# Loading x ahead of the small constants, and splitting four channel blocks at a time, in a hybrid trunk kernel

## The chip, the cores and the metric

The kernel runs on one core of a Trainium2 chip. The time is the device time of one execution in microseconds (us); the median of several executions counts. The profile names the engines PE (matmul; PEld its weight loads), DVE (vector), ACT (activation), POOL and SP. SP here does little but issue DMAs.

## The reference

One layer of an encoder, on x of 1024 tokens by 1024 channels, in fp32. Three head groups share one input projection; their results go through one output projection, and a gated feed-forward follows.

```python
h = rmsnorm(x, pre_mix_norm[l])
proj = h @ w_in[l]
(a_q, a_k, a_v, s_z, s_xbc, s_dt, g_qkv, g_z, g_b, g_a) = jnp.split(proj, offs, axis=-1)
att = swa_sink_alibi(a_q, a_k, a_v, attn_sinks[l])
ssd = ssd_mixer(s_z, s_xbc, s_dt, ssd_conv_w[l], ssd_conv_b[l], ...)
gdn = gdn_mixer(g_qkv, g_z, g_b, g_a, gdn_conv_w[l], gdn_dt_bias[l], gdn_A_log[l], gdn_norm_w[l])
mix = jnp.concatenate([att, ssd, gdn], axis=-1) @ w_out[l]
x = x + rmsnorm(mix, post_mix_norm[l])
h = rmsnorm(x, pre_ffn_norm[l])
f = (jax.nn.silu(h @ ffn_w_gate[l]) * (h @ ffn_w_up[l])) @ ffn_w_down[l]
...
```

`rmsnorm` divides each row by the root of its mean square and multiplies channel by channel with a weight. `gdn_mixer` and `ssd_mixer` run q, k, v and x, B, C through a causal convolution of four taps and SiLU, and form decays exp of cumulated sums from g_a and s_dt.

## The kernel before

The 1024 tokens go through the mixers in two halves of 512 (four tiles of 128 rows, t = 0 to 3). A half's normed rows are turned so that channels lie on partitions: eight blocks (k = 0 to 7) of 128 channels by 512 tokens. Every fp32 operand of the large products is split into a rounded part and a rest (names with `hhi` and `hlo` for activations, `wh` and `wl` for weights, `wr` for the raw weights), and three matmuls stand for one product (`gemm`, `gemm_rows`, L203 to L215).

The opening (`load_norm(0)`, L290 to L321) loads x tile by tile, squares and sums each row on ACT (L253), takes the power -1/2 on POOL (`rsq`, L167), scales the row on DVE (L317), and `split_T` transposes 32 pieces on PE (L231, `tp_a`), multiplies them by the norm's weight as a column (`ncol`, itself turned on PE at L120) and splits them, a block at a time, with 24 ACT (L236) and 24 DVE instructions (L237). `STEPS` has tiles 0 and 1 go alone and 2 and 3 together. Then `load_rest` loads the small constants from SP's queue: masks, biases, norm weights (`nw_in`), and the convolution taps (`cw_gdn`, `cw_ssd`), which PE turns into `pt_conv` (L158) and ACT copies to `wconv` (L159).

The first half then runs the steps of `ORD[0]`. K begins with `decay_block`: `gate_rows` makes `mm_gz`, 96 matmuls of 272 columns, and a chain of small instructions turns the decay inputs into `da`, `cs_ps`, `cs`, `chl`, `tp_cs`, `csT` and then, per pair of tiles, `D_g`, `D_s` and the exponentials `E_g`, `E_s` (L453). Then `conv_block` runs for gk, gq, gk, gq: a product of 24 matmuls of 512 columns into one of two PSUM banks `mm`, its copy `cb_` (L344), an ACT instruction that scales it by the last tap (L348, it needs `wconv`) into `kq`, three DVE multiply-adds (L350), tanh and product. mm_gv, mm_B, mm_C, mm_x and mm_z follow. Step N, late in the half, normalises the second half's rows, whose x has been loaded and scaled in the opening.

A scheduler orders each engine's instructions at build time, in the priority of the code, and `tc.high_priority()` moves a weight piece's load and split forward. An engine then takes its instructions strictly in that order. Buffers come from pools with a fixed number of tiles: `cb` has two, `wr` three, `nat` four, `mm` two banks.

Of the kernel before, what the change touches and what calls it, by code (L numbers as in the profile page):

```python
# [8 lines left out]
F32 = mybir.dt.float32  # L9
# [7 lines left out]
P = 128  # L17
# [16 lines left out]
STEPS = (1, 1, 2)  # L34
# [35 lines left out]
def trunk(ctx, tc, a):  # L70
# [47 lines left out]
    def load_columns():  # L118
        pt = mx("pt_ncol", "gd")
        pe.transpose(pt[:, 0:8], nw8[:, 0:P], ident[0:8, 0:8])  # L120
        vec.tensor_copy(ncol[:, 0:8], pt[:, 0:8])

    def load_rest():
# [6 lines left out]
        dma(row12[:, 0, 4:12], a["ssd_dt_bias"].to_broadcast([P, 8]))  # L130
        dma(row12[:, 0, 0:4], a["gdn_dt_bias"].to_broadcast([P, 4]))
        dma(row12[:, 1, 4:12], a["ssd_A_log"].to_broadcast([P, 8]))
        dma(row12[:, 1, 0:4], a["gdn_A_log"].to_broadcast([P, 4]))
        dma(dskip, a["ssd_D"].to_broadcast([P, 8]))
        dma(sinks, a["attn_sinks"].to_broadcast([P, 4]))
# [3 lines left out]
        dma(nw[0:8, 0:P], a["pre_ffn_norm"][0].rearrange("(k p) -> k p", p=P))  # L139
        dma(nw[10:14, 0:P], a["ssd_norm_w"][0].rearrange("(k p) -> k p", p=P))  # L140
        for i in range(4):
            dma(nw[14 + i // 2:15 + i // 2, (i % 2) * 64:(i % 2 + 1) * 64], a["gdn_norm_w"])
# [5 lines left out]
        for nm, b0, c0 in (("gdn", 8, 0), ("gdn", 11, 384), ("ssd", 0, 0), ("ssd", 4, 512)):  # L148
            n = 3 if nm == "gdn" else 4
            cw = cpool.tile([P, HT + 3], F32, tag="cb", name=f"cw_{nm}{c0}")  # L150
            if nm == "gdn":
                pool.memset(cw[0:5, 0:n * P], 0.0)
            dma(cw[0:4, 0:n * P], a[f"{nm}_conv_w"][0][:, c0:c0 + n * P])
            if nm == "ssd":
                dma(cw[4:5, 0:n * P], a["ssd_conv_b"][:, c0:c0 + n * P])
# [17 lines left out]

    def split_piece(name, n, width, hi, lo, fill):
# [4 lines left out]
        with tc.high_priority():  # L179
            raw = wpool.tile([P, WC], F32, tag="wr", name=f"wr_{name}")  # L180
# [35 lines left out]

    def split_alloc(name, hp):
        return [(hp.tile([P, HT], F32R, tag="hhi", name=f"hhi_{name}{k}", bufs=KB),
                 hp.tile([P, HT], F32R, tag="hlo", name=f"hlo_{name}{k}", bufs=KB))
                for k in range(KB)]  # L220
# [69 lines left out]
    def load_norm(h):  # L290
        def load(t):
            xt = npool.tile([P, D], F32, tag="nat", name=f"x_{h}{t}")
            r0 = h * HT + t * P
            dma(xt, x_in[r0:r0 + P])
            return xt

        xts = []
        with tc.high_priority():
            for t in range(NT):
                if h == 0 and t == 2:  # L300
                    break
                xts.append(load(t))
                if h == 0 and t == 0:
                    dma(nw8[:, 0:P], a["pre_mix_norm"][0].rearrange("(k p) -> k p", p=P))
        for t in range(len(xts), NT):
            xts.append(load(t))
        hT = split_alloc(f"a{h}", hpool)
        if h == 0:
            load_columns()
        t0 = 0  # L310
        for step in STEPS if h == 0 else (NT,):
            nats = []
            for xt in xts[t0:t0 + step]:
                r = rms_scale(xt)
                for g in range(2):
                    s = slice(g * HT, (g + 1) * HT)
                    vec.tensor_scalar(xt[:, s], xt[:, s], r, None, op0=ALU.mult)  # L317
# [55 lines left out]

    def decay_block(h, hT):
# [416 lines left out]
    def half(h, hT, order):  # L791
# [3 lines left out]
        def keys():  # L795
            sc = st["sc"] = decay_block(h, hT)
            kq = [kqpool.tile([P, 2, HT], F32, tag="kq", name=f"kq{h}{b}") for b in range(2)]
            for b in range(2):
                conv_block(h, hT, f"gk{b}", O_G + 256 + b * P, 10 + b, kq[b][:, 0])
                conv_block(h, hT, f"gq{b}", O_G + b * P, 8 + b, kq[b][:, 1])  # L800
            st["grp"] = []
# [57 lines left out]
        def after():  # L859
            st["next"] = load_norm(h + 1)  # L860
# [101 lines left out]

    hT = load_norm(0)
    load_rest()
    for h in range(2):
        for t in range(GT):
            dma(vds[h][t].rearrange("h (b r) j -> (h b r) j", b=4).rearrange("(x r) j -> x r j", r=32)[:, 16:32, 0:16],
                S_bd[0:16].rearrange("p b l -> p (b l)")[:, 0:256].rearrange("p (r j) -> p r j", r=16))
# [398 lines left out]
```

## Time and profile before

| | us |
|---|---|
| median of three runs | 1269.42 |
| lowest and highest | 1267.31, 1270.78 |
| the profiled execution, its time | 1268.95 |
| its span in the trace | 1267.2 |
| PE busy | 1218.1 |
| DVE busy | 913.7 |
| ACT busy | 574.8 |
| POOL busy | 217.8 |

The span runs from the first to the last instruction; 1.75 us of the execution lie outside. A line of the trace gives start and duration, the engine, the line of code, the operation with the tiles that it writes and reads, and in brackets how long the engine had been idle and who released it. L-numbers in the profile are those of the kernel that ran.

### The profile page before, as it was taken

What the parts mean: (1) busy time and instruction counts of PE and PEld (TensorE: products, weight loads), DVE (VectorE), ACT (ScalarE), POOL (GpSimd) and SP (SyncE); (2) the same over time, 40 slices, a digit from 0 to 9 for tenths busy, and PEclk for the clock granted to TensorE, in tenths of its full rate; (3) what the DMA queues carried; (4) which work ended last, traced back from release to release, by engine and by line L of the source; (5) the groups of instructions that cost most, each with busy time, mean ns of one, the idle gap of its engine ahead of it and who ended that gap; (6) DMA issues with size and microseconds to landing.
All of it is one profiled execution on the core that took longest, in us unless ns stands there. A gap on an engine that the chain in (4) does not pass through costs nothing.

```text
span 1267.2 us, 18619 instructions
## 1 busy us (share of the span) xinstructions
PE 1218.1 (96%) x6384; PEld 1005.0 (79%) x6384; DVE 913.7 (72%) x1850; ACT 574.8 (45%) x1245; POOL 217.8 (17%) x313
## 2 busy tenths in 40 slices
PE   5999999999998999889999999999999999999997
PEld 4878778987787889878877888888888887888885
DVE  5677865796797385654668999886677666768885
ACT  7464435456443453553546443333433334444661
POOL 3244454233355432100000000000000000000000
PEclk9999989999998999979999999999999999999998
DMA  7333432143333222464573554542333367676315
GB/s 224 94 78 63 102 78 70 49 117 92 73 90 68 85 86 73 126 224 127 161 232 103 191 190 164 182 155 72 117 108 108 108 244 271 188 238 205 94 57 199
DMA packets 181795, 168.15 MB, mean 133 GB/s; under 512 B 52510, under 2 KB 137018, under 8 KB 181700
## 3 DMA queue, kind: packets, MB, share of 16 engines
q1 hardware_dynamic: 164276, 133.14, 36.0%
q10 hardware_dynamic: 17424, 33.82, 7.3%
q8 instruction: 50, 0.82, 0.3%
q14 instruction: 45, 0.37, 0.1%
HBM read 126.82 MB, written 40.11 MB: 132 GB/s over the span
## 4 chain that ended last, share of the span: by engine, by line
PE 82%; DVE 8%; DMA 6%; ACT 2%; issue 1%; SPq 1%; POOL 0%; ACTq 0%; DVEq 0%; POOLq 0%
PE mm_p L1238 5%; PE mm_p L1239 5%; PE mm_p L1240 5%; DMA wr_e<-in_ffn_w_gate_dram 1%; DMA x<-in_x_dram 1%; PE mm_o L208 1%; PE gram L490 1%; PE mm_o L209 1%; DMA yb<-in_ffn_w_down_dram 1%; PE mm_o L207 1%; PE y L703 1%; PE as L746 1%; PE ao L782 1%; PE mm_z L207 1%; DVE Tpr L538 1%
## 5 line engine op out<-in xcount | busy, mean ns | idle before, releaser
L167 POOL TENSOR_TENSOR rsq<-ssv,mhalf 128x1 f32<-128x1 f32 x32 | 20.0, 628 | 750.9 <-DVE ssv L260 740.3
L208 PE MATMUL mm_z<-wl_z,hhi_a 128*128 128x256 f32 x128 | 37.3, 291 | 1.6 <-DVE wl_z L184 1.6
L207 PE MATMUL mm_z<-wh_z,hhi_a 128*128 128x256 f32 x128 | 38.8, 303 | 0.0
L209 PE MATMUL mm_z<-wh_z,hlo_a 128*128 128x256 f32 x128 | 37.3, 291 | 0.0
L208 PE MATMUL mm_o<-wl_wo,hhi_m 128*128 128x256 f32 x128 | 36.7, 287 | 0.0
L209 PE MATMUL mm_o<-wh_wo,hlo_m 128*128 128x256 f32 x128 | 36.3, 284 | 0.0
L207 PE MATMUL mm_o<-wh_wo,hhi_m 128*128 128x256 f32 x128 | 36.3, 284 | 0.0
L183 ACT ACTIVATE wh_wo<-wr_wo 128x512 fp32r<-128x512 f32 x30 | 18.7, 631 | 27.2 <-PE mm_o L1133 8.2
L184 DVE TENSOR_TENSOR wl_wo<-wr_wo,wh_wo 128x512 fp32r<-128x512 f32 x22 | 15.2, 692 | 18.0 <-ACT wh_wo L183 17.9
L208 PEld LDWEIGHTS mm_z<-wl_z,hhi_a 128*128 128x128 f32 x128 | 25.6, 200 | 2.1 <-DVE wl_z L184 1.9
L207 PEld LDWEIGHTS mm_z<-wh_z,hhi_a 128*128 128x128 f32 x128 | 25.7, 201 | 0.7
L703 PE MATMUL y<-xs,E_s 128*128 128x64 f32 x128 | 19.1, 290 | 7.3 <-DVE E_s L696 7.3
L215 PE MATMUL mm_x<-hhi_a,wl_x 128*128 128x512 f32 x64 | 26.0, 406 | 0.0
L214 PE MATMUL mm_x<-hlo_a,wh_x 128*128 128x512 f32 x64 | 25.5, 398 | 0.0
L209 PEld LDWEIGHTS mm_z<-wh_z,hlo_a 128*128 128x128 f32 x128 | 25.4, 199 | 0.0
L213 PE MATMUL mm_x<-hhi_a,wh_x 128*128 128x512 f32 x64 | 25.3, 395 | 0.0
L703 PEld LDWEIGHTS y<-xs,E_s 128*128 128x128 f32 x128 | 18.1, 208 | 8.7 <-DVE E_s L696 7.7
L208 PEld LDWEIGHTS mm_o<-wl_wo,hhi_m 128*128 128x128 f32 x128 | 24.1, 189 | 1.0 <-issue 1.0
L209 PEld LDWEIGHTS mm_o<-wh_wo,hlo_m 128*128 128x128 f32 x128 | 24.1, 189 | 0.3 <-issue 0.3
L207 PEld LDWEIGHTS mm_o<-wh_wo,hhi_m 128*128 128x128 f32 x128 | 24.1, 188 | 0.3 <-ACT apT L772 0.3
L1131 PE MATMUL mm_o<-wh_wo,mhi 128*128 128x512 f32 x56 | 22.0, 393 | 0.3 <-ACT mhi L236 0.3
L207 PE MATMUL mm_gz<-wh_gz,hhi_a 128*128 128x272 f32 x64 | 20.8, 325 | 1.3 <-ACT dtn L378 1.3
(1801 smaller groups left out, 4380.8 us busy)
## 6 DMA issues: line engine op xcount, KB each, us to landing
wr_wo<-in_w_out_dram SPq DMA_DIRECT2D x32, 256.0 KB
x<-in_x_dram SPq DMA_DIRECT2D x8, 512.0 KB
wr_x<-in_w_in_dram SPq DMA_DIRECT2D x16, 256.0 KB
wr_z<-in_w_in_dram SPq DMA_DIRECT2D x16, 256.0 KB
res<-in_x_dram SPq DMA_DIRECT2D x8, 512.0 KB
resf<-x1d SPq DMA_DIRECT2D x8, 512.0 KB
mixn<-mixd SPq DMA_DIRECT2D x12, 256.0 KB
wr_e<-in_ffn_w_gate_dram SPq DMA_DIRECT2D x12, 256.0 KB
```

Source lines behind the costliest of these rows:

```text
L167: pool.tensor_tensor(r[:, 0:n], v, mhalf[:, 0:n], op=ALU.pow)
L207: pe.matmul(ps, hi[:, tsl], whi, start=k == 0, stop=False)
L208: pe.matmul(ps, hi[:, tsl], wlo, start=False, stop=False)
L209: pe.matmul(ps, lo[:, tsl], whi, start=False, stop=k == len(wp) - 1)
L213: pe.matmul(ps, whi, hi, start=k == 0, stop=False)
L214: pe.matmul(ps, whi, lo, start=False, stop=False)
L215: pe.matmul(ps, wlo, hi, start=False, stop=k == len(wp) - 1)
L703: pe.matmul(yd[:, j], E[j], xs[:, j], start=True, stop=True)
L1131: pe.matmul(ps[t], hi[:, s], whi, start=k == korder[0], stop=False)
L1238: pe.matmul(ps[j], ah[:, s], bh, start=i == 0, stop=False)
L1239: pe.matmul(ps[j], ah[:, s], bl, start=False, stop=False)
L1240: pe.matmul(ps[j], al[:, s], bh, start=False, stop=i == NP - 1)
```

## The change

Six things change.

First, `load_first` replaces `load_norm(0)`. The four x tiles go to buffers that only later stages use, all four are loaded ahead of the weights, and the norm's weight is loaded as a row, broadcast to all partitions (`pn_row`, two of 256 KB). A row is multiplied by its own scale and by that row in one DVE instruction, in place. Four blocks of a tile are transposed into one PSUM tile, one ACT copy makes `hhi` and one DVE subtraction `hlo`, 8 each instead of 24. The split tiles hold four blocks each, everywhere (`split_alloc`, `xtile`).

Second, the second half's x is loaded and scaled in step N; a copy of one column from a tile of the V step holds it back.

Third, the gz weights of the first half use the `nat` buffers, and the weight pieces of K in the first half are not moved forward (`ahead`, `raw_of`).

Fourth, `load_rest` and the eight clears `vd` are called after gz, from `decay_block`.

Fifth, in `load_rest` the biases, norm weights and taps are issued from POOL's queue, 17 DMAs.

Sixth, `STEPS` goes.

```diff
     def load_rest():
+        dma(nw8[:, 0:P], a["pre_mix_norm"][0].rearrange("(k p) -> k p", p=P))
         pt = mx("pt_ncol", "gd")
...
-        dma(row12[:, 0, 4:12], a["ssd_dt_bias"].to_broadcast([P, 8]))
+        nc.gpsimd.dma_start(row12[:, 0, 4:12], a["ssd_dt_bias"].to_broadcast([P, 8]))
...
         pool.memset(nw[0:16, 0:P], 1.0)
-        dma(nw[0:8, 0:P], a["pre_ffn_norm"][0].rearrange("(k p) -> k p", p=P))
+        nc.gpsimd.dma_start(nw[0:8, 0:P], a["pre_ffn_norm"][0].rearrange("(k p) -> k p", p=P))
...
-            dma(cw[0:4, 0:n * P], a[f"{nm}_conv_w"][0][:, c0:c0 + n * P])
+            nc.gpsimd.dma_start(cw[0:4, 0:n * P], a[f"{nm}_conv_w"][0][:, c0:c0 + n * P])
...
-        with tc.high_priority():
-            raw = wpool.tile([P, WC], F32, tag="wr", name=f"wr_{name}")
+        with ahead[0]():
+            raw = raw_of[0](f"wr_{name}")
...
+        hi, lo = [[hp.tile([P, 4, HT], F32R, tag=tg, name=f"{tg}_{name}{k}", bufs=2) for k in range(2)]
+                  for tg in ("hhi", "hlo")]
+        four[:] = [hi, lo]
+        return [(hi[k // 4][:, k % 4], lo[k // 4][:, k % 4]) for k in range(KB)]
...
+    def load_first():
+
+        rows = [rpool.tile([P, HT], F32, tag=f"row{g}", name=f"pn_row{g}") for g in range(2)]
+        xts = []
+        for t in range(NT):
+            xt, start = load_x(t, mpool, ("sE", "Wst")[t // 2], 2)
+            with tc.high_priority():
+                start()
+                if t == 1:
+                    for g in range(2):
+                        dma(rows[g], a["pre_mix_norm"][:, g * HT:(g + 1) * HT].to_broadcast([P, HT]))
+            xts.append(xt)
+        hT = split_alloc("a0", hpool)
+        hi, lo = four
+        for t, xt in enumerate(xts):
+            with tc.high_priority():
+                r = rms_scale(xt)
+                s = slice(t * P, (t + 1) * P)
+                for g in range(2):
+                    q = xt[:, g * HT:(g + 1) * HT]
+                    stt(out=q, in0=q, scalar=r, in1=rows[g], op0=ALU.mult, op1=ALU.mult)
+                    p = mx(f"tp_a{t}{g}", ("gd", "sd", "at", "mm")[(2 * t + g) % 4]).rearrange("p (k c) -> p k c", k=4)
+                    for k in range(4):
+                        pe.transpose(p[:, k], q[:, k * P:(k + 1) * P], ident)
+                    act(out=hi[g][:, :, s], in_=p, func=AF.Copy)
+                    vec.tensor_tensor(lo[g][:, :, s], p, f32(hi[g][:, :, s]), op=ALU.subtract)
+        return hT
...
+            xt, start = load_x(h * NT + t, npool, "nat")
+            vec.tensor_copy(xt[:, 0:1], hold[:, 0:1])
+            start()
...
+        usual = raw_of[0]
+        if h == 0:
+            raw_of[0] = lambda nm: npool.tile([P, D], F32, tag="nat", name=nm)
         gz = gate_rows(h, hT, "gz", [(0, w_in[:, O_GZ:O_GZ + 264]), (264, w_in[:, O_DT:O_DT + 8])], 272,
                        lambda t, ps: act(out=dtn[:, t, :], in_=ps[:, 256:272], func=AF.Copy))
+        raw_of[0] = usual
+        if h == 0:
+            load_rest()
+            clear_inverse()
...
-            st["next"] = load_norm(h + 1)
+            st["next"] = load_norm(h + 1, st["v"][0])
...
-    hT = load_norm(0)
-    load_rest()
+    hT = load_first()
     hT = half(0, hT, ORD[0])
```

The order in which instructions stand on an engine shows where things went. On PE before, between the end of the first mm_gq and the second mm_gk there is nothing; the numbers in the names tell tiles apart.

```order
L213 MATMUL mm_gq00_659<-hhi_a07_191,wh_gq004_653 128x512
L214 MATMUL mm_gq00_659<-hlo_a07_192,wh_gq004_653 128x512
L215 MATMUL mm_gq00_659<-hhi_a07_191,wl_gq004_654 128x512
L213 MATMUL mm_gk10_706<-hhi_a00_177,wh_gk100_694 128x512
L214 MATMUL mm_gk10_706<-hlo_a00_178,wh_gk100_694 128x512
```

On PE after, these stand at the same place, from the last matmul of mm_gq to the first of the second mm_gk (xN: N alike in a row).

```order
L216 MATMUL mm_gq00_619<-hhi_a01_181,wl_gq004_614 128x512
L475 MATMUL D_g000_749<-mask_r_95,ident_r_94 128x512
L142 MATMUL pt_ncol2_460<-cst_90,nw_in_452 128x16
L156 MATMUL pt_conv_464<-cst_90,cw_gdn0_465 128x5 x3
L446 MATMUL cs_ps0_532<-da0_530,cst_90 128x48
L465 MATMUL tp_cs0_551<-cst_90,chl0_548 24x128 x4
L479 MATMUL D_g000_749<-csT0_556,sel_r_96 128x256 x2
L479 MATMUL D_s0001_1801<-csT0_556,sel_r_96 128x256 x2
L156 MATMUL pt_conv_464<-cst_90,cw_gdn384_471 128x5 x3
L156 MATMUL pt_conv_464<-cst_90,cw_ssd0_477 128x5 x4
L156 MATMUL pt_conv_464<-cst_90,cw_ssd512_484 128x5 x4
L214 MATMUL mm_gk10_666<-hhi_a00_180,wh_gk100_654 128x512
```

The masks of D_g and D_s, pt_ncol2 and pt_conv stood inside gz before; cs_ps, tp_cs and the products with csT stood after the second mm_gk had begun. In between, and not shown, stand the further masks and products of the same kind.

On ACT before, the first mm_gk's bank is emptied (cb_gk, kq) right behind the splits of the next weights; D_g's exponentials come some twenty instructions later.

```order
L394 ACTIVATE e0_547<-ay0_545 128x48
L183 ACTIVATE wh_gk104_700<-wr_gk104_702 128x512
L183 ACTIVATE wh_gq100_741<-wr_gq100_743 128x512
L344 ACTIVATE cb_gk00_637<-mm_gk00_612 128x512
L348 ACTIVATE kq00_598<-mm_gk00_612,wconv_98 128x512
```

On ACT after, the decay chain and 16 exponentials stand ahead of it; wconv, which before was copied inside gz, is copied between.

```order
L184 ACTIVATE wh_gv000_1019<-wr_gv000_1021 128x512
L454 ACTIVATE ecs0_538<-cs0_535 128x48
L467 ACTIVATE csT0_556<-tp_cs0_551 24x512
L484 ACTIVATE E_g00_748<-D_g000_749,ncs0_537 128x128 x4
L484 ACTIVATE E_g00_748<-D_g001_757,ncs0_537 128x128 x4
L484 ACTIVATE E_s000_1792<-D_s0000_1793,ncs0_537 128x128 x4
L484 ACTIVATE E_s000_1792<-D_s0001_1801,ncs0_537 128x128 x4
L362 ACTIVATE cb_gk00_597<-mm_gk00_572 128x512
L157 ACTIVATE wconv_98<-pt_conv_464 128x70
L362 ACTIVATE cb_gq00_644<-mm_gq00_619 128x512
L366 ACTIVATE kq00_558<-mm_gk00_572,wconv_98 128x512
```

On POOL, which issued no DMA before, these stand after the split of the second mm_gk's weights. Six other DMAs (biases, A_log, D, sinks) stand at POOL's start, and between the last three rows, not shown, stand the DMAs of cw_gdn384 and cw_ssd512's taps and one product.

```order
L136 MEMSET nw_in_452 16x128
L137 DMA nw_in_452<-in_pre_ffn_norm_dram 8x128
L138 DMA nw_in_452<-in_ssd_norm_w_dram 4x128
L140 DMA nw_in_452<-in_gdn_norm_w_dram 1x16x4 x4
L150 MEMSET cw_gdn0_465 5x384
L185 TENSOR_TENSOR wl_gq100_702<-wr_gq100_703,wh_gq100_701 128x512
L151 DMA cw_gdn0_465<-in_gdn_conv_w_dram 4x384
L185 TENSOR_TENSOR wl_gv000_1020<-wr_gv000_1021,wh_gv000_1019 128x512
L150 MEMSET cw_gdn384_471 5x384
L151 DMA cw_ssd0_477<-in_ssd_conv_w_dram 4x512
L153 DMA cw_ssd0_477<-in_ssd_conv_b_dram 1x16x32
L153 DMA cw_ssd512_484<-in_ssd_conv_b_dram 1x16x32
```

What SP issued in the opening before, ahead of the second half's x, is now issued by POOL around and after the first mm_gk; the tap buffers come from the two `cb` tiles, so each load there waits until PE has read the one before it.

More of the change, by code (lines that the diff above doesn't have):

```diff
@@ new lines, in load_norm @@
+    def load_norm(h, hold):
+        nats = []
+        for t in range(NT):
+            xt, start = load_x(h * NT + t, npool, "nat")
+            vec.tensor_copy(xt[:, 0:1], hold[:, 0:1])
+            start()
+            r = rms_scale(xt)
+            for g in range(2):
+                s = slice(g * HT, (g + 1) * HT)
+                vec.tensor_scalar(xt[:, s], xt[:, s], r, None, op0=ALU.mult)
+            nats.append(cols_of(xt))
+        hT = split_alloc(f"a{h}", hpool)
+        split_T(f"a{h}", nats, 0, hT, 0)
@@ L795, in keys @@
         def keys():
+            if h == 0:
+                ahead[0] = ExitStack
             sc = st["sc"] = decay_block(h, hT)
@@ L800, in keys @@
                 conv_block(h, hT, f"gq{b}", O_G + b * P, 8 + b, kq[b][:, 1])
+            ahead[0] = tc.high_priority
             st["grp"] = []
```

72 lines of the change are left out of this document (25 added, 47 removed).

## The prediction

> **What bounds the kernel now.** I read the page first, then PE's waits in the opening, then windows there, then the order of PE's own instructions. On the page, PE is busy 96% of the span, and of 40 slices only the first is far from full.
>
> ```profile
> span 1267.2 us, 18619 instructions
> PE 1218.1 (96%) x6384; PEld 1005.0 (79%) x6384; DVE 913.7 (72%) x1850; ACT 574.8 (45%) x1245; POOL 217.8 (17%) x313
> PE   5999999999998999889999999999999999999997
> ```
>
> So time can be won in the first 32 us, or by work that PE no longer does; and a wait on PE that is new almost anywhere else adds its full length. The waits of PE in the first 60 us (reason, total, times, longest) say what the opening consists of: 8.1 us until anything can be transposed, 4.2 us for scaled rows, 2.0 us for a split.
>
> ```profile
> PE pt_ncol L120 <- DMA wr_gz<-in_w_in_dram: 8.1, 1, 8.1
> PE tp_a L231 <- DVE x L317: 4.2, 2, 3.6
> PE D_g L444 <- DVE hlo_a L237: 2.0, 1, 2.0
> ```
>
> The windows give busy time and instructions of PE, PEld, DVE, ACT and POOL, then the granted clock, DMA share and GB/s. Loads run at 305 to 337 GB/s at the start; between 65 and 140 us PE is busy for the whole 75 us. A delay that reaches 65 us can't be made good before 140.
>
> ```profile
> 0.00:5.00 5.00, 0.00 (x0) 0.00 (x0) 0.00 (x0) 1.72 (x3) 1.01 (x7) 1.00 0.56 169
> 5.00:10.00 5.00, 1.91 (x9) 1.75 (x9) 2.27 (x6) 3.32 (x8) 2.15 (x4) 1.00 1.07 305
> 10.00:15.00 5.00, 1.39 (x8) 1.15 (x7) 3.30 (x12) 4.29 (x15) 2.25 (x2) 1.00 1.02 337
> 25.00:30.00 5.00, 2.79 (x13) 2.40 (x13) 3.02 (x10) 2.26 (x7) 0.36 (x2) 0.78 0.97 280
> 30.00:35.00 5.00, 3.70 (x27) 3.20 (x25) 3.07 (x10) 2.62 (x9) 1.10 (x2) 0.88 0.40 130
> 65.00:140.00 75.00, 75.00 (x388) 59.55 (x388) 56.27 (x133) 40.05 (x90) 33.07 (x53) 1.00 0.36 83
> ```
>
> PE's timeline (start, duration, line, tiles) gives the marks by which I reckon: mm_gz ends and the first mm_gk begins at 41.63, mm_gq at 47.19, the second mm_gk at 52.77, mm_gv at 65.51. The last gz matmul holds PE for 0.12 us until the next begins. The windows from 25 to 35 us, where the 2.0 us of idle lies, show a granted clock of 0.78 and 0.88: a lack of 0.22 over 5 us is 1.1 us, and 0.12 over the next five 0.6: this wait cost 1.7 us beside its own length.
>
> ```profile
> 41.51 0.29 PE L209 MATMUL mm_gz<-wh_gz,hlo_a 128*128 128x272 f32 x1
> 41.63 0.39 PE L213 MATMUL mm_gk<-hhi_a,wh_gk 128*128 128x512 f32 x1
> ...
> 47.19 0.39 PE L213 MATMUL mm_gq<-hhi_a,wh_gq 128*128 128x512 f32 x1
> ...
> 52.77 0.39 PE L213 MATMUL mm_gk<-hhi_a,wh_gk 128*128 128x512 f32 x1
> ...
> 62.73 0.60 PE L434 MATMUL tp_cs<-cst,chl 128*24 128x128 f32 x4
> ...
> 65.51 0.50 PE L213 MATMUL mm_gv<-hhi_a,wh_gv 128*128 128x512 f32 x1
> 68.70 0.73 PE L448 MATMUL D_g<-csT,sel_r 24*128 24x256 f32 x4
> ```
>
> **Part 1: gz comes earlier.** Ahead of the first scaling stand 64 KB of cst, 2048 KB of x and 512 KB of norm row, 2.69 MB. The first window moved 0.85 MB; the other 1.84 MB at 320 GB/s take 5.8 us, so the row is there at 10.8. DVE then has in its order, up to the last scaling, 8 scalings, 2 of the 8 subtractions and one weight split. A two-input 128x512 on DVE is nearest to the kq convolution, 0.75 us; the split costs 1.07.
>
> ```profile
> L350 DVE SCALAR_TENSOR_TENSOR kq<-cb_gk,wconv,kq 128x512 f32<-128x512 f32 x6 | 4.5, 748 | 1.2 <-ACT kq L348 1.2
> L184 DVE TENSOR_TENSOR wl_gz<-wr_gz,wh_gz 128x544 fp32r<-128x544 f32 x2 | 2.1, 1074 | 0.6 <-ACT wh_gz L183 0.5
> L237 DVE SCALAR_TENSOR_TENSOR hlo_a<-tp_a,ncol,hhi_a 128x128 fp32r<-128x128 f32 x16 | 5.0, 344 | 1.6 <-ACT hhi_a L236 1.6
> L317 DVE TENSOR_SCALAR x<-x,rsq 128x512 f32<-128x512 f32 x16 | 8.2, 553 | 3.3 <-POOL rsq L167 2.5 <-DMA pm_row<-in_post_mix_norm_dram 0.7
> 8.27 1.97 PE L231 MATMUL tp_a<-cst,x 128*128 128x128 f32 x8
> ```
>
> That is 10.8 + 10 x 0.75 + 1.07 = 19.4. All 32 transposes stand ahead of mm_gz, so gz can't start sooner; the last four, about 0.25 us each (8 in 1.97 us, below), add 0.9, to 20.3. The 96 gz matmuls take 0.12 to 0.13 each, 12.0, and a start at the low clock adds 1.7, as above: 34.0. For handing pieces between ACT and DVE I add 1.5, near the 1.6 that DVE idled for ACT at its 16 small splits. gz ends at **35.5** instead of 41.6, a gain of 6.1 us. The gains of fewer, larger evictions (8 + 8 for 24 + 24) are inside this sum, on ACT and DVE.
>
> **Part 2: what gz's end then runs into.** mm_gk and mm_gq take 52.77 - 41.63 = 11.1 us, so they end at 46.6. Before, the second mm_gk followed without a gap, because the tap table wconv was ready by then and ACT emptied the first mm_gk's bank at once. After, the second mm_gk needs that bank, whose last reader needs wconv; and in ACT's order that reader stands behind the decay chain and 16 exponentials, in PE's the last pt_conv stands behind the decay transposes. There are two chains, worked out with an issue cost c and a landing time L for a DMA on POOL, of which before has none.
>
> ```profile
> 42.81 0.41 DVE L364 SCALAR_TENSOR_TENSOR gz<-gth_gz,mm_gz 128x256 f32<-128x256 f32 x1
> ...
> 57.51 0.20 DVE L420 COPY cs<-cs_ps 128x48 f32<-128x48 f32 x1
> ...
> 59.09 0.20 DVE L431 TENSOR_TENSOR chl<-cs,chl 128x48 fp32r<-128x48 f32 x1
> ...
> 47.69 0.58 ACT L344 ACTIVATE cb_gk<-mm_gk 128x512 f32<-128x512 f32 x1
> 48.17 0.77 ACT L348 ACTIVATE kq<-mm_gk,wconv 128x512 f32<-128x512 f32 x1
> ...
> 63.36 0.59 ACT L436 ACTIVATE csT<-tp_cs 24x512 fp32r<-24x512 f32 x1 [1.20 <-PE tp_cs L434]
> ...
> 69.24 2.18 ACT L453 ACTIVATE E_g<-D_g,ncs 128x128 f32<-128x128 f32 x8 [0.26 <-PE D_g L448]
> ```
>
> *L.* ACT's timeline and SP's below give cst: issued at 0.73, its reader starts at 2.74, so 2.0 us. The upper end is x, 512 KB, issued at 1.17 and read at 4.88: 3.7 us. I take 2.0, since these transfers are at most 8 KB.
>
> *c.* The lowest row is SP's small issue, 0.27; POOL's cheapest own arithmetic is 0.63 a time, its 128x512 subtraction 1.30. I take **0.95**, the middle of the two POOL rows, as the issue is now POOL's work, and keep 0.27 and 1.30.
>
> ```profile
> 2.74 0.31 ACT L127 ACTIVATE ident_r<-cst 128x128 fp32r<-128x128 f32 x1 [0.74 <-DMA cst<-in_consts_dram]
> 4.88 0.63 ACT L253 ACTIVATE junk<-x 128x512 bf16<-128x512 f32 x1 [1.82 <-DMA x<-in_x_dram]
> ...
> 0.73 0.39 SPq L104 DMA_DIRECT2D cst<-in_consts_dram  x1
> 1.17 0.42 SPq L294 DMA_DIRECT2D x<-in_x_dram  x1
> 17.34 0.27 SPq L140 DMA_DIRECT2D nw_in<-in_ssd_norm_w_dram  x1
> ...
> L167 POOL TENSOR_TENSOR rsq<-ssv,mhalf 128x1 f32<-128x1 f32 x32 | 20.0, 628 | 750.9 <-DVE ssv L260 740.3
> L184 POOL TENSOR_TENSOR wl_gq<-wr_gq,wh_gq 128x512 fp32r<-128x512 f32 x2 | 2.6, 1295 | 9.7 <-ACT wh_gq L183 9.7
> ```
>
> The Trainium skill (DMA: Bandwidth & Descriptors, Latency and other measured facts) puts the first byte of a DMA from this queue at about 1 us against 0.6 us from SP's. Were c an estimate by that page, 1.0, the second mm_gk would start some 0.6 us later than I say below; no run here shows it yet.
>
> *POOL's chain.* ctmp gets its buffer when the last gz product has read it, 1.6 us after gz's end as before (42.81 + 0.41 against 41.63): 37.1. Issue 0.4 and landing 2.0 bring 39.5, two copies on ACT and a memset 0.7: 40.2. Six norm-weight DMAs, 6c = 5.7: 45.9. A memset, which I take at 0.4, and a weight split 1.30: 47.6. cw_gdn's DMA: 48.6, landed 50.6. POOL meanwhile does another split and a memset, to 50.3, and three DMAs, to 53.2, landed 55.2. Then pt_conv reads them, which frees the buffer of the last two DMAs: 55.8 + 1.9 + 2.0 = 59.7. pt_conv, wconv (0.5), the copy between them in ACT's order (0.5) and kq (0.77): the bank is free at 61.5.
>
> *The decay chain* is behind cw_gdn on PE, at 50.6. cs_ps follows, by 51.4; from cs to chl it is 59.29 - 57.51 = 1.8; from tp_cs to csT's end 63.95 - 62.73 = 1.2; from D_g to its exponential 0.54. That is 54.9. 16 exponentials, twice 2.18, end at 59.3, and cb_gk, wconv, cb_gq and kq (2.0) at 61.3. So the two are level, and the second mm_gk starts at **61.4**.
>
> At c = 0.27 it would be 58.2, since the decay chain then starts at mm_gq's end and the masks (47.8) and is 10.4 long from there; at c = 1.30, 65.3; and with L = 3.7 besides, three landings in a row, 70.4.
>
> **The sum.** Second mm_gk 61.4 instead of 52.8: +8.6. After a wait this long PE starts at the low clock as behind the 2.0 us: +1.7. What PE did behind this place and now does inside the gap: tp_cs 0.6, and csT's products of D_g and D_s, 0.73 each: -2.1. Together **+8.2 us**, which then stays on PE through the full window to 140 and, as DVE waited too, beyond. The profiled execution took 1268.95 us (span 1267.2 and 1.75 around it), 0.5 under the median of the three runs, 1269.42. The forecast is 1268.95 + 8.2 = **1277**. Between c = 0.27 and 1.30 it goes from 1274.0 to 1281.1; gz's end may be off by 2 us either way, so the case spans 1272 to 1283.
>
> Of the other edits I cost at nothing: the second half's x (four loads, squares and scalings between 75 and 105, where DVE was busy 56 of 75 us; were that cover gone, 8 scalings of 0.553 us, 4.4); the clears that move, on SP only; tiles of four blocks instead of one in the later stages, whose weight pieces are split only five steps ahead (WS) anyway, so that coarser tiles change which load comes first and not PE's order.
>
> **The rivals.**
>
> *POOL's transfers are dearer than any row.* For it: 12 issues of the chain stand on an engine between its own splits. By 1.30 and 3.7 it gives 1268.95 + 17.6 - 0.4, about 1286. The Trainium skill (SBUF — State Buffer, the paragraph on the DVE blocks DMA trap) has such a transfer starved while DVE copies between SBUF places: 0.62 us becomes 3.1. By it the same rival would be what to expect where DVE is busy. But DVE itself waits for wconv in most of this gap, which speaks against. Chance 0.16.
>
> *The gain at the start doesn't come:* the 32 transposes ahead of gz wait for the last x row, and gz ends at 41.6 as before. Every later mark slides by 6.1: 1283. Against: the sum of DVE has 6 us to spare. Chance 0.06.
>
> *The lost time is taken back at later waits.* PE now waits 1.65 us for a weight split and 2.87 for E_s; the first E_s is now computed 100 us sooner.
>
> ```profile
> 157.70 0.38 PE L208 MATMUL mm_z<-wl_z,hhi_a 128*128 128x256 f32 x1 [1.65 <-DVE wl_z L184]
> 164.24 1.91 PE L703 MATMUL y<-xs,E_s 128*128 128x64 f32 x8 [2.87 <-DVE E_s L696]
> ```
>
> Both gone: 1277.2 - 4.5 = 1272.7; with the same for E_s elsewhere, less. Against: DVE, which releases both, is held by the same gap. Chance 0.14.
>
> *Faster:* the chain isn't on the path, the second mm_gk follows mm_gq at 46.6, and the 6.1 us of part 1 are kept: 1262.8. It decides from the point where kq has left the first bank by 46.6, so wconv by about 45. For it: nothing but the orders of ACT and PE ties the first bank to the decay chain, so shorter steps there would show at once; against: even the cheapest c leaves 58.2. Chance 0.11.
>
> **How the numbers follow.** Forecast 0.53, the rivals 0.16, 0.06, 0.14 and 0.11. Likeliest 1277, its own range 1272 to 1283. A measurement of this kernel tells 0.3%, 3.8 us, from no change: 1265.6 to 1273.2. Slower: the forecast less its lowest part, 0.49, and 0.22, about 0.71. Same: 0.14 and the 0.04 = 0.18. Faster 0.11. The range reaches from between the faster case and the same one, 1266, to the dear one's 1286, leaving out some 0.18.
>
> **What would show it.** Right: PE idle for 10 to 18 us between mm_gq and the second mm_gk with ACT's kq as releaser; gz ended near 35.5; a granted clock below 0.9 right after the gap; DVE idle in it. Wrong: no such gap; gz's end after 39; POOL's issue rows under 0.4 us; or a later stage, the down products above all, whose marks move apart by over 3 us from those before.

## The result, and the profile after

The changed kernel took 1280.15 us (median of 4, 1275.41 to 1281.81) against 1268.37 for the kernel before in the same runs: a ratio of 1.0106 (95% interval 1.0077 to 1.0136), slower by about 12 us. On another chip it was 1.0090 (1.0066 to 1.0113). The profiled execution is the fastest of the four, 1275.41 us, and so shows only half of the loss.

The page of the changed kernel: PE's busy time is 4 us less than before, the span 6.4 us longer, and a queue for POOL's transfers is new.

```profile
span 1273.6 us, 18550 instructions
PE 1214.4 (95%) x6384; PEld 1002.3 (79%) x6384; DVE 913.5 (72%) x1838; ACT 571.7 (45%) x1229; POOL 226.5 (18%) x331
...
q0 software_dynamic: 576, 0.06, 0.2%
```

PE's timeline of the changed kernel has the marks of the prediction: transposes from 14.3, gz from 25.4, its end and the first mm_gk at 37.5, mm_gq at 43.3 with its end at 49.0, then one small step after another, and the second mm_gk at 60.2.

```profile
14.30 3.30 PE L321 MATMUL tp_a<-cst,x 128*128 128x128 f32 x16 [14.30 <-DVE x L318]
...
25.36 0.39 PE L208 MATMUL mm_gz<-wh_gz,hhi_a 128*128 128x272 f32 x1 [1.40 <-DVE hlo_a L323]
...
37.47 0.39 PE L214 MATMUL mm_gk<-hhi_a,wh_gk 128*128 128x512 f32 x1
...
43.28 0.50 PE L214 MATMUL mm_gq<-hhi_a,wh_gq 128*128 128x512 f32 x1
...
48.97 0.62 PE L475 MATMUL D_g<-mask_r,ident_r 128*128 128x512 f32 x2
...
57.80 0.56 PE L156 MATMUL pt_conv<-cst,cw_ssd 5*128 5x5 f32 x4 [2.25 <-DMA cw_ssd<-in_ssd_conv_b_dram]
60.21 0.80 PE L214 MATMUL mm_gk<-hhi_a,wh_gk 128*128 128x512 f32 x1 [1.85 <-ACT kq L366]
...
74.51 0.47 PE L214 MATMUL mm_gv<-hhi_a,wh_gv 128*128 128x512 f32 x1
```

So gz ended 4.2 us sooner than before (41.63), and the second mm_gk began 7.4 later (52.77), mm_gv 9.0 later (65.51). From mm_gq's end to the second mm_gk it is 11.2 us. PE is idle for 6.1 of them, in five waits, of which the last, for kq, is 1.85 us; the rest are small products. POOL's timeline has the new issues. They take 0.53 to 0.58 us each (the four of nw_in together 1.96), and the last, issued at 55.96, is what PE reads at 57.80: 1.84 us to land.

```profile
42.32 0.20 POOL L136 MEMSET nw_in<- 16x128 f32 x1 [0.69 <-ACT sel_r L127]
42.81 0.58 POOL L137 DMA_DIRECT2D nw_in<-in_pre_ffn_norm_dram  x1 [0.29 <-POOL nw_in L136]
43.38 0.53 POOL L138 DMA_DIRECT2D nw_in<-in_ssd_norm_w_dram  x1
43.90 1.96 POOL L140 DMA_DIRECT2D nw_in<-in_gdn_norm_w_dram  x4
...
47.48 0.53 POOL L151 DMA_DIRECT2D cw_gdn<-in_gdn_conv_w_dram  x1
...
55.42 0.54 POOL L151 DMA_DIRECT2D cw_ssd<-in_ssd_conv_w_dram  x1 [2.38 <-PE pt_conv L156]
55.96 0.54 POOL L153 DMA_DIRECT2D cw_ssd<-in_ssd_conv_b_dram  x1
```

ACT's timeline shows the other chain: 16 exponentials until 58.2, then the copies, and kq, which frees the bank, at 60.2. The last pt_conv ends at 58.36 and ACT is free for wconv at 58.65, so the two chains end within 0.3 us of each other.

```profile
54.16 2.17 ACT L484 ACTIVATE E_g<-D_g,ncs 128x128 f32<-128x128 f32 x8 [0.59 <-PE D_g L479]
56.17 2.23 ACT L484 ACTIVATE E_s<-D_s,ncs 128x128 f32<-128x128 f32 x8
58.17 0.71 ACT L362 ACTIVATE cb_gk<-mm_gk 128x512 f32<-128x512 f32 x1
58.65 0.35 ACT L157 ACTIVATE wconv<-pt_conv 128x70 f32<-128x70 f32 x1
...
59.24 0.92 ACT L366 ACTIVATE kq<-mm_gk,wconv 128x512 f32<-128x512 f32 x1
```

The windows of the changed kernel show the clock: 0.50 from 56 to 64 us, 0.89 in the next four. The second mm_gk took 7.8 us, where the first of before took 5.6 and its second 6.0 with the cs_ps products inside. DVE did nothing from 56 to 60.

```profile
52.00:56.00 4.00, 2.53 (x19) 2.16 (x19) 0.20 (x2) 2.67 (x10) 1.60 (x5) 0.83 0.30 70
56.00:60.00 4.00, 0.56 (x4) 0.50 (x4) 0.00 (x0) 4.00 (x15) 1.10 (x5) 0.50 0.03 7
60.00:64.00 4.00, 3.79 (x9) 3.02 (x10) 3.73 (x6) 1.05 (x3) 0.00 (x0) 0.50 0.01 2
64.00:68.00 4.00, 4.00 (x16) 3.20 (x16) 2.42 (x4) 1.69 (x4) 0.20 (x2) 0.89 0.06 9
```

Behind this the distance to before doesn't stay at 9. At mm_B it is 7.3, since products of D_g and D_s that stood ahead of mm_B before are done already. At the first mm_z it is 118.3 against 111.7, +6.6, at mm_aq 180.4 against 175.5, +4.9, and at 405 us of before 4.0. Two waits shrank. Here is the sum of PE's waits after 100 us, first before, then after.

```profile
PE y L703 <- DVE E_s L696: 7.3, 2, 4.4
...
PE mm_z L208 <- DVE wl_z L184: 1.6, 1, 1.6
...
PE mm_p L1238 <- ACT wh_p1B L927: 1.0, 1, 1.0
```

```profile
PE y L734 <- DVE E_s L727: 5.7, 2, 4.5
...
PE mm_p L1272 <- ACT wh_p1B L961: 1.9, 1, 1.9
...
PE mm_z L208 <- DVE z L382: 0.6, 1, 0.6
```

The waits of mm_z and of y for E_s shrank by 1.0 and 1.6 us. Two waits of D_s, for ssd_st and y, grew by 1.8 together, so the waits alone don't explain what was given back.

Late in the kernel two more steps appear. The transposes `tp_f`, which wait for a split of DVE, are 1.8 us further behind at 555 us of before, but this is made up by 659, where the distance is 4.1. The first of the down products, near 1052, loses 2.5 us to its loads and to the clock behind the wait. That makes the 6.5 us of this execution.

The second profile of the same kernel, an execution of 1280.29 us, is nearer to the median and gives another picture. mm_gz began at 25.45 as here, but gz ran more slowly (the clock was 0.50 from 24 to 28 us, here 1.00) and ended 1.4 us later. The second mm_gk was 8.9 late, mm_gv 10.3 and the first mm_x (98.66 before) 8.6, and almost nothing was given back: 8.5 at mm_aq, 8.2 at 1043. The first down product added 3.0.

### The profile page after: what moved, and what is told of

The parts are those of the page before. It is cut to its first block, busy times and chain, and to the rows that moved or that the text cites. A ratio compares the mean times of both kernels' runs of the same rounds, so it can differ in the third digit from the quotient of the medians.

```text
span 1273.6 us, 18550 instructions
## 1 busy us (share of the span) xinstructions
PE 1214.4 (95%) x6384; PEld 1002.3 (79%) x6384; DVE 913.5 (72%) x1838; ACT 571.7 (45%) x1229; POOL 226.5 (18%) x331
## 4 chain that ended last, share of the span: by engine, by line
PE 84%; DVE 6%; DMA 5%; ACT 2%; issue 1%; POOL 1%; SPq 1%; ACTq 0%; DVEq 0%; POOLq 0%
PE mm_p L1273 5%; PE mm_p L1274 5%; PE mm_p L1272 5%; DMA wr_e<-in_ffn_w_gate_dram 1%; PE mm_o L209 1%; PE mm_o L208 1%; PE mm_o L210 1%; PE gram L521 1%; PE as L777 1%; PE y L734 1%; PE mm_z L208 1%; PE ao L813 1%; PE mm_x L214 1%; PE mm_z L210 1%; PE mm_z L209 1%
## 5 line engine op out<-in xcount | busy, mean ns | idle before, releaser
L209 PEld LDWEIGHTS mm_z<-wl_z,hhi_a 128*128 128x128 f32 x128 | 24.5, 191 | 0.3
L321 PE MATMUL tp_a<-cst,x 128*128 128x128 f32 x32 | 6.8, 392 | 17.2 <-DVE x L318 17.2
```

The lines of the kernel that those rows point to most:

```text
L209: pe.matmul(ps, hi[:, tsl], wlo, start=False, stop=False)
```

## The experiments

Each kernel was compared with the kernel before on its own chip. Those of one group ran on the same chip.

| kernel | median, us | ratio to before | 95% interval |
|---|---|---|---|
| rest_early_sp | 1280.8 | 1.0112 | 1.0082 to 1.0142 |
| rest_early_pool | 1281.84 | 1.0131 | 1.0092 to 1.0169 |
| rest_late_sp | 1272.32 | 1.0049 | 1.0030 to 1.0068 |
| before_four | 1272.12 | 1.0043 | 1.0024 to 1.0062 |
| after_again | 1278.18 | 1.0090 | 1.0066 to 1.0113 |
| six_sp | 1274.33 | 1.0060 | 1.0038 to 1.0083 |
| after_two | 1278.47 | 1.0092 | 1.0068 to 1.0116 |
| before_xfirst | 1265.6 | 0.9991 | 0.9975 to 1.0007 |
| early_nohold | 1271.01 | 1.0030 | 1.0016 to 1.0043 |
| late_sp_again | 1272.66 | 1.0040 | 1.0024 to 1.0056 |
| xf_clear | 1268.11 | 1.0005 | 0.9990 to 1.0020 |
| xf_clear22 | 1264.69 | 0.9981 | 0.9967 to 0.9995 |

### First group: the place, the queue, or the tiles

**rest_early_sp** takes the constants back ahead of the first half and onto SP's queue.

```diff
-        if h == 0:
-            load_rest()
-            clear_inverse()
...
     hT = load_first()
+    load_rest()
+    clear_inverse()
...
-        nc.gpsimd.dma_start(row12[:, 0, 4:12], a["ssd_dt_bias"].to_broadcast([P, 8]))
+        dma(row12[:, 0, 4:12], a["ssd_dt_bias"].to_broadcast([P, 8]))
...
```

> The changed kernel with the constants and the clears called right behind load_first, ahead of the first half, and issued by SP as before. Theory A, the place (masks, taps and the decay chain stand between mm_gq and the second mm_gk because the constants come after gz): the second mm_gk follows mm_gq without a gap, at 49 to 53 us; time 1262 to 1269, some 3 us under before to level with it. Theory B, the queue (POOL's DMAs are what is slow): the same, so this run alone doesn't tell A from B. Theory C, the tiles of four blocks lose the time late in the kernel: the opening gains, but the time stays above 1272.

The opening did as theory A said: PE runs from gz to mm_gq and on to the second mm_gk without a stop, and mm_C begins at 87.6 against 89.7 before. But the time is 15 us over before, a miss for theories A and B; only theory C's number fits, and the loss isn't late in the kernel, where C has it. It sits at the end of the first phase: the product mm_o begins at 472.7, before at 461.7. The windows of this kernel show why:

```profile
456.00:460.00 4.00, 2.62 (x15) 2.19 (x16) 4.00 (x13) 2.42 (x8) 2.75 (x5) 0.83 0.02 4
460.00:464.00 4.00, 4.00 (x15) 2.94 (x15) 3.62 (x12) 0.96 (x3) 1.26 (x3) 0.50 0.00 0
464.00:468.00 4.00, 4.00 (x19) 3.82 (x18) 1.51 (x5) 1.63 (x4) 0.54 (x1) 0.50 0.10 33
468.00:472.00 4.00, 4.00 (x21) 4.00 (x21) 1.64 (x4) 0.00 (x0) 0.73 (x1) 0.50 0.01 2
472.00:476.00 4.00, 4.00 (x21) 4.00 (x21) 3.71 (x13) 1.11 (x2) 0.00 (x0) 0.53 0.61 197
```

From 460 to 475 PE is shown busy throughout and at half clock. Before, the same windows have a clock of 1.00, as in this one:

```profile
464.00:468.00 4.00, 4.00 (x57) 3.96 (x55) 3.11 (x12) 1.00 (x5) 2.16 (x4) 1.00 0.33 134
```

That is worth some 7 us, an estimate from half a clock over 15 us. Two things differ from the changed kernel there: the scheduler orders the first phase otherwise (of the 3900 matmuls ahead of the feed-forward some 850 stand elsewhere), and the queue of the constants.

**rest_early_pool** is the same with the 17 small DMAs on POOL.

> As rest_early_sp, but the 17 small DMAs stay on POOL's queue. Theory A: within 2 us of rest_early_sp, since 0.52 us for an issue and 1.8 us to land are hidden behind gz. Theory B: PE still waits for pt_conv or kq by 5 us or more before the second mm_gk, and the time is 1273 or more.

1.0131 against 1.0112, inside both intervals: level with rest_early_sp, as theory A said, though both carry the loss just named, so that they tell little of the gap. This run has POOL's queue and the same stretch at half clock (0.50 from 472 to 484 us), so the queue isn't its cause. PE's wait for its first transpose is 14.1 us here against 11.1. Nor are the issues hidden, as theory A had it. In the profiled execution, one of two at 1290 us (the other four took 1279.6 to 1282.1), PE waits for the scaled rows of the last two tiles:

```profile
26.26 1.11 PE L321 MATMUL tp_a<-cst,x 128*128 128x128 f32 x4 [8.53 <-DVE x L318]
```

POOL's `rsq` for these rows stands behind six issues of nw_in (16.2 to 19.2 us), and on DVE two weight splits, the second until 24.5, stand ahead of the scaling.

**rest_late_sp** leaves the constants behind gz and takes the 17 DMAs to SP's queue (`nc.gpsimd.dma_start` becomes `dma` in `load_rest`).

> The changed kernel with the 17 small DMAs on SP's queue, at the changed place behind gz. Theory A: the decay chain and 16 exponentials still stand ahead of the first kq, so the second mm_gk starts at 56 to 60 us instead of 60.2, and the time is 1274 to 1281. Theory B: the second mm_gk starts below 52 and the time is 1262 to 1268.

The mechanism is that of theory A: PE waits 4.0 us for ACT's kq, and the second mm_gk begins at 57.65.

```profile
57.65 0.80 PE L214 MATMUL mm_gk<-hhi_a,wh_gk 128*128 128x512 f32 x1 [3.99 <-ACT kq L366]
```

From gz's end that is 23.7 us, against 22.7 in the changed kernel: the decay chain and the exponentials alone make the gap. The time is below what I gave it, 1272.3. So the gap of the changed kernel stands whatever the queue, and POOL's queue has a price of its own: 0.5% between this kernel and the changed one.

**before_four** is the kernel before with `split_alloc` and `xtile` of the change.

```diff
-        return [(hp.tile([P, HT], F32R, tag="hhi", name=f"hhi_{name}{k}", bufs=KB),
...
+        hi, lo = [[hp.tile([P, 4, HT], F32R, tag=tg, name=f"{tg}_{name}{k}", bufs=2) for k in range(2)]
+                  for tg in ("hhi", "hlo")]
...
-        return hpool.tile([P, HT], F32, tag=("hhi", "hlo")[i % 2], name=f"{nm}{i}", bufs=KB)
+            xcur[0] = hpool.tile([P, 4, HT], F32, tag=("hhi", "hlo")[nx[0] % 2], name=f"{nm}{i}", bufs=2)
+        return xcur[0][:, i % 4]
```

> The kernel before with the tiles of four blocks (split_alloc and xtile of the change), nothing else. Theory A: within 0.3% of before, 1265 to 1272. Theory C: 1272 to 1277, with the first of the down products waiting longer for its loads, 1.9 us or more instead of 1.0 near 1052 us, and a lower clock behind it.

1.0043: theory C is right here in time and wait, and the edit that I had costed at nothing takes 5.5 us by itself. The wait of the first down product is 2.1 us instead of 1.0; a lower clock behind it, which I also expected, did not come. PE's windows show the wait, in before and then in before_four.

```profile
1050.00:1055.00 5.00, 4.00 (x18) 2.97 (x17) 3.27 (x7) 3.23 (x6) 0.00 (x0) 1.00 1.08 401
1055.00:1060.00 5.00, 5.00 (x24) 4.03 (x23) 4.96 (x9) 2.31 (x4) 0.00 (x0) 1.00 0.96 331
```

```profile
1050.00:1055.00 5.00, 3.77 (x17) 2.67 (x15) 3.22 (x6) 0.29 (x1) 0.00 (x0) 1.00 1.05 402
1055.00:1060.00 5.00, 4.08 (x18) 3.33 (x19) 4.62 (x8) 4.10 (x8) 0.00 (x0) 1.00 1.06 402
```

The transfers run at some 400 GB/s in both during the wait, so what comes when is decided by the order of the loads. ACT's timeline of before_four names the load that is late, in the middle of the wait:

```profile
1054.71 0.63 ACT L930 ACTIVATE wh_p1A<-p1x 128x512 fp32r<-128x512 f32 x1 [5.23 <-DMA yb<-in_ffn_w_down_dram]
```

ACT sat for a load of the next product's weights (`yb`). PE's products are 2.3 us later here than before at this place, but SP issues the eight loads of yb 3.8 us later (from 1046.31 instead of 1042.48), and the eight loads of p1x into the x buffers 4.4 us later (from 1028.44 instead of 1024.07). The code suggests why, though no run shows it alone: an x buffer that comes free four blocks at a time lets SP load less far ahead.

Of the 5.5 us the profiled execution shows 3.5 by this stage: 2.5 at the end of gz, where a tile of four blocks is likely waited for longer, and 1.2 at the first down product, less 0.2 between; 2.3 us lost at tp_f are made up by 659. The rest isn't placed, since the traced execution of before took 1268.95, over this chip's median of 1265.77. The 2.5 us arose in an opening that the change replaces, so the 5.5 can't simply be added to the changed kernel's other costs.

### Second group: what POOL's queue costs

**after_again** is the changed kernel.

> The changed kernel once more, on the same chip as the three kernels beside it. Theory D, three separate costs: tiles of four blocks (about 5 us, as before_four showed), the gap ahead of the second mm_gk (about 4 us after what later waits give back), and POOL's queue (5 us and more in most executions, not in the one profiled first): 1.0 to 1.2% over before. Theory E, POOL's queue costs nothing of its own: 0.5 to 0.7% over before, as rest_late_sp.

1.0090: under theory D's 1.0 to 1.2%, but nearer to it than to theory E's 0.5 to 0.7%.

**six_sp** moves the six broadcast DMAs at POOL's start to SP's queue.

```diff
-        nc.gpsimd.dma_start(row12[:, 0, 4:12], a["ssd_dt_bias"].to_broadcast([P, 8]))
...
-        nc.gpsimd.dma_start(sinks, a["attn_sinks"].to_broadcast([P, 4]))
+        dma(row12[:, 0, 4:12], a["ssd_dt_bias"].to_broadcast([P, 8]))
...
+        dma(sinks, a["attn_sinks"].to_broadcast([P, 4]))
```

> The changed kernel with only the six broadcast DMAs at POOL's start (biases, A_log, D, sinks: 768 packets) on SP's queue, behind gz; the other 11 stay on POOL. If these six disturb the loading of x at the start: the first scaled row 2 us earlier or more (PE's first transpose below 12.5 us instead of 14.3) and at least 4 us under after_again. If the 11 later ones are what costs: within 2 us of after_again.

3.9 us under after_again, just short of the 4 expected. The first transpose comes 3.0 us sooner, at 11.4, and gz begins at 21.4 instead of 25.4. ACT's timeline shows when the second x tile is there, and DVE's when the norm row is, in the changed kernel:

```profile
10.07 0.63 ACT L257 ACTIVATE junk<-x 128x512 bf16<-128x512 f32 x1 [2.97 <-DMA x<-in_x_dram]
...
13.49 1.41 DVE L318 SCALAR_TENSOR_TENSOR x<-x,rsq,pn_row 128x512 f32<-128x512 f32 x2 [1.57 <-DMA pn_row<-in_pre_mix_norm_dram]
```

and in six_sp:

```profile
7.69 0.63 ACT L257 ACTIVATE junk<-x 128x512 bf16<-128x512 f32 x1 [1.38 <-DMA x<-in_x_dram]
...
10.62 1.41 DVE L318 SCALAR_TENSOR_TENSOR x<-x,rsq,pn_row 128x512 f32<-128x512 f32 x2 [1.07 <-DMA pn_row<-in_pre_mix_norm_dram]
```

The windows from 5 to 10 us show the rate, the changed kernel first: the DMA engines are busy, and move a third less.

```profile
5.00:10.00 5.00, 0.00 (x0) 0.00 (x0) 0.31 (x2) 1.45 (x4) 0.86 (x2) 1.00 0.98 223
```

```profile
5.00:10.00 5.00, 0.00 (x0) 0.00 (x0) 0.62 (x4) 3.49 (x11) 0.92 (x2) 1.00 0.86 337
```

On the page of the changed kernel, shown above, POOL's queue has 576 packets, which took 0.2% of the sixteen DMA engines' span, by estimate some 40 us of engine time. In six_sp it has almost none:

```profile
q0 software_dynamic: 384, 0.04, 0.0%
```

Six transfers of 2 to 4 KB each, spread over 128 partitions, thus hold up 2.7 MB of x and norm row by 2.9 us at the norm row, on which the first scaling waits. The run moves them to another queue and to a later time at once, so it doesn't tell which of the two helps. The other eleven, still on POOL here, cost what is left between six_sp (1.0060) and rest_late_sp (1.0049 and 1.0040): 0.1 to 0.2%, inside the intervals.

**after_two** has tiles of two blocks.

```diff
-        hi, lo = [[hp.tile([P, 4, HT], F32R, tag=tg, name=f"{tg}_{name}{k}", bufs=2) for k in range(2)]
+        hi, lo = [[hp.tile([P, 2, HT], F32R, tag=tg, name=f"{tg}_{name}{k}", bufs=4) for k in range(4)]
...
+                    for m in range(2):
...
```

> The changed kernel with tiles of two blocks instead of four everywhere; 16 evictions each on ACT and DVE in the opening instead of 8, transposes as in the change. Theory D: the first down product waits about 1.0 us again near 1050 and the late loss goes: 2 to 4 us under after_again, less about 1 us for the opening. If the size of the tiles is no cause: level with after_again or slower by 1 to 2.

Level with after_again: the wait of the first down product did fall, to 1.5 us from 2.4, and its loss to 0.6 from 3.0. The longer opening (the first mm_x 9.7 late instead of 8.6) took about 1 us of that, and at 659 us, behind tp_f, the kernel is 1.7 further behind than after_again. Half the size removed most of the loss at the down products, and as much was lost elsewhere.

**before_xfirst** loads all four x tiles of the first half first, and no longer moves the gz weights and the second half's x forward.

```diff
-                if h == 0 and t == 2:
+                if h == 1:
                     break
...
-        with tc.high_priority():
+        with ahead[0]():
...
+        if h == 0:
+            ahead[0] = ExitStack
         gz = gate_rows(h, hT, "gz", ...
+        ahead[0] = tc.high_priority
```

> The kernel before with only this: all four x tiles of the first half are loaded first, and the gz weights aren't moved forward, so that SP issues x ahead of weights and constants. Theory: the waits for scaled rows (4.2 us) and for the split (2.0) shrink, gz ends at 36 to 39 us instead of 41.6, and nothing stands ahead of the second mm_gk: 0.2 to 0.5% under before. Rival: the gz weights now come behind the small constants on SP and the wait only moves to them: gz ends at 41 or later, within 0.2% of before or slower.

No change that can be told, 0.9991. gz ended at 39.15 instead of 41.63, between the two theories, and by the down products 0.4 us of it was left (the same matmul of mm_p at 1080.86 against 1081.21). The gz weights were issued from 16.5 to 24 us, behind the constants and the clears.

### Third group: the gap without the other costs, and a better version

**early_nohold** is rest_early_sp without `vec.tensor_copy(xt[:, 0:1], hold[:, 0:1])`.

> rest_early_sp without the copy that holds the second half's x back: constants ahead of the first half on SP's queue, x of the second half free to load early, tiles of four blocks. On PE its order from mm_gk on is that of before. Theory: rest_early_sp was slow because of the order that the scheduler made of the first half's end when both the gap and the early x were gone, so this one loses that: 10 us and more under rest_early_sp's ratio, and with no gap the opening gains 2 to 4 us, which the tiles give back: 0.0 to 0.3% over before. Rival, the gap costs nothing by the end, since later waits give it back: 0.4 to 0.6% over before, as rest_late_sp.

**late_sp_again** is rest_late_sp.

> rest_late_sp once more, beside early_nohold on the same chip: it has the gap, and the same tiles. Theory: 0.3 to 0.6% over before and 2 to 5 us over early_nohold. Rival: level with early_nohold within 1 us.

1.0030 and 1.0040. early_nohold lost the 10 us of rest_early_sp: mm_gv begins at 64.8, 0.7 sooner than before, with no stop ahead of the second mm_gk, and only some 90 of the 3900 matmuls stand elsewhere than before. Holding x back doesn't cost the 10 us by itself, since rest_late_sp and the changed kernel do it too; what is left is the order. Against late_sp_again, which has the gap (second mm_gk at 58.1, 5.3 late), early_nohold is 1.7 us better by the medians, less than expected and within the intervals. In the time of the whole kernel the two rivals are not told apart.

The traces tell more. At the first mm_x, where the work that moved into the gap is made up for, the profiled executions are later than before by

| kernel | us at the first mm_x |
|---|---|
| changed kernel, two executions | 7.2, 8.6 |
| six_sp | 4.1 |
| rest_late_sp, late_sp_again | 4.8, 4.3 |
| early_nohold | 0.0 |

So at this place the gap is worth 4 to 5 us against early_nohold, and the six broadcasts on POOL 3 to 4 more. What is left of it at 1043 us depends on the execution: 4.4 in rest_late_sp, nothing (0.4 ahead) in late_sp_again, which is the same kernel; 4.1 and 8.2 in the changed one. There the first down product adds 1.2 to 3.0 us in every kernel with tiles of four blocks, 0.6 with tiles of two, and nothing with tiles of one block.

**xf_clear** moves the eight clears behind gz in before_xfirst; **xf_clear22** has `STEPS = (2, 2)` besides.

```diff
+        if h == 0:
+            clear_inverse()
...
-STEPS = (1, 1, 2)
+STEPS = (2, 2)
```

> before_xfirst with the eight clears moved behind gz in the code, so that SP issues the gz weights some 2 to 4 us sooner; tiles of one block, constants on SP ahead of gz. If the gz weights bound before_xfirst (SP issued them at 16.5 to 24 us, behind the clears): gz ends at 36 to 38 us, 0.1 to 0.4% under before. If not: as before_xfirst, within 0.15% of before.

> xf_clear with the first half's tiles split in two steps of two tiles instead of 1, 1 and 2: 16 evictions on ACT and on DVE instead of 24. If DVE and ACT bound the opening once x is there early: 0.5 to 2 us under xf_clear. If the first transposes matter, which now wait for the second tile: 1 to 2 us over it.

xf_clear has gz begin at 16.7, but end at 41.3, later than before_xfirst and than the 36 to 38 expected. Its windows tell it:

```profile
15.00:20.00 5.00, 4.00 (x16) 2.87 (x15) 4.43 (x12) 5.00 (x16) 1.34 (x1) 0.50 0.71 157
20.00:25.00 5.00, 5.00 (x35) 4.73 (x34) 2.76 (x9) 2.62 (x7) 3.01 (x3) 0.86 0.74 169
25.00:30.00 5.00, 3.63 (x27) 2.83 (x25) 1.39 (x3) 1.34 (x3) 0.00 (x0) 1.00 0.86 217
30.00:35.00 5.00, 3.06 (x15) 2.97 (x16) 1.14 (x5) 3.27 (x12) 0.55 (x1) 0.67 1.00 385
35.00:40.00 5.00, 5.00 (x29) 5.00 (x29) 2.17 (x10) 3.02 (x9) 1.21 (x3) 0.65 0.10 39
```

An earlier start was spent at a clock of 0.50, and again at 0.67 and 0.65 behind the next wait (3.3 us, for the taps). xf_clear22 is the fastest kernel here, 0.9981 (0.9967 to 0.9995), a little faster than before and 3.4 us under xf_clear, where 2 was the most expected. Its opening gains little (mm_gv 0.6 us sooner than before); its profile is ahead of before by 2.0 at mm_aq and by 4.6 at the down products. Why the rest of the kernel runs ahead was not tried, and one profile can't tell it: the two of rest_late_sp's kernel lie 4.8 us apart at 1043.

## Why the prediction was right or wrong

It said 1277, slower; it was 1280.15, slower, and the gap stood where it was said to stand. By its steps:

| step | said | the profiled execution showed |
|---|---|---|
| norm row loaded | 10.8 | 13.5 (10.6 in six_sp) |
| gz's end | 35.5 | 37.5 (34.6 in six_sp) |
| mm_gq's end | 46.6 | 49.0 |
| c and L of POOL's DMAs | 0.95 and 2.0 | 0.53 to 0.58, and 1.84 |
| the second mm_gk | 61.4 | 60.2 |
| half clock behind it | 1.7 | 2.2 (7.8 us instead of 5.6) |
| lateness after it | 8.2 | 7.3 at mm_B, behind the work that moved (8.6 in the second profile) |
| that it stays | whole | 4.1 left at 1043 in one execution, 8.2 in the other |
| tiles of four blocks | 0 | 2.5 and 3.0 at the first down product; 5.5 alone (before_four) |

**Right in mechanism: the gap.** Both chains reached wconv within 0.3 us of each other, as said, and rest_late_sp shows the decay chain making the gap without POOL. c was mis-sized: the row that was nearest is POOL's cheapest operation, 0.63, or SP's issue, not the middle to 1.30. Had I taken 0.55, the decay chain alone would have decided, and the second mm_gk would have come out at 58.2, some 3 us sooner; gz ended 2 us later than said. The two errors nearly cancelled in this mark, which is luck. At c = 1.30, besides, the twelve issues give 65.6 and not 65.3, which moves the upper end by 0.3.

**The signs.** A clock below 0.9, an idle DVE and kq as the last releaser came as said. PE's idle time did not: 6.1 us of a gap of 11.2, not 10 to 18. One sign of being wrong came to its edge: the down products moved apart by 2.5 us in one execution and 3.0 in the other, where over 3 was to count.

**Wrong in part 1: the loading rate.** The 320 GB/s were read from a kernel whose queue had the opening to itself. The six broadcast DMAs from POOL, which the text named only as standing at POOL's start, brought it to 223, and six_sp put 3.9 us on them. That is the term of the sum that was left out. With the six moved, the row comes at 10.6 and gz ends at 34.6, both within 1 us of what was said. In the changed kernel gz began at 25.4, some 3.6 us after the sum's start, but ran at full clock and did not need the 1.7 us.

**Wrong in the last paragraph of part 2: the coarser tiles cost nothing.** The reason given, that pieces are split only five steps ahead, looks at the splits and not at the loads, which in `before` run up to sixteen tiles ahead, one at a time. before_four measured 0.43% for the tiles alone in the kernel before, about as much as POOL's queue (0.5%, rest_late_sp against the changed kernel). The down products are the part that all kernels with such tiles share.

**The rival of the lost time taken back** came true in one execution and not in the other. In the first the opening's 7.3 us shrank to 4.1, in the second, nearer to the median, 8.6 stayed at 8.2. There the forecast's 8.2 is what the opening cost, and the 3.0 of the down products leads from 1277 to 1280. But the 8.2 is in part luck: the broadcasts, which it lacked, stand in it for an issue time that was too dear.

**The dear POOL transfers.** An issue took half of what I made of it, and the landing 1.84 us. The Trainium skill (DMA: Bandwidth & Descriptors, Latency and other measured facts) gives about 1 us for the first byte; no run here shows the first byte apart from the landing. By the Trainium skill (SBUF — State Buffer, the paragraph on the DVE blocks DMA trap) such transfers starve while DVE copies. No run here shows it: the issues at 43 us, with DVE busy in small steps, and at 55 us, with DVE idle, took 0.53 and 0.54 us. The price that POOL's queue did have came from another side, the load rate.

How the opening's gap divides from the later x loading is left open: no run has the one without the other at the same order of the first phase.

## What to carry to other kernels

Ask of every moved load what is queued behind the instruction that reads it, on each engine: here two chains ended at one bank. And ask of every tile that is made larger when its buffer comes free: here the same bytes in fewer pieces cost 0.43%, part of it in a stage that the edit wasn't about. When a scheduler orders the work, compare the order in the untouched part as well, since an edit in the opening put some 850 matmuls elsewhere here.

## What the runs showed of the hardware

Small broadcast DMAs from POOL's queue slowed large ones from SP's: 223 GB/s instead of 337 from 5 to 10 us, with the DMA engines busy at 0.98. The POOL queue's packets took 0.2% of the sixteen engines' span with the six broadcasts and 0.0% without them.

PE can be shown busy all the time and stay at half clock: from 460 to 472 us in rest_early_sp, three windows of 4.00 of 4 at 0.50. The matmuls there were of 64 to 256 columns, some on half the rows; the clock came back 3 us after the dense mm_o began at 472.65, where its matmuls go from 0.41 to 0.28 us. The Trainium skill (TensorE: Matmul & The Clock Gate, What's actually happening) gives some 3.4 us of sustained work to get back to full clock. Behind the gap in the changed kernel the trace agrees as far as it took no less: some 4.4 us, from 60.2 until the matmuls of 0.63 us end at 64.7. In rest_early_sp 12 us shown as busy did not bring it back, so there the trace's busy time was not what the gate counted.
